# A scan kernel on one core: the Fourier branch's steps at other places of the turn, its loads in one batch a turn

## The chip, the cores and the metric

The kernel runs on one core of a Trainium2 chip. The metric is device time in microseconds (us) of one execution. Five engines work side by side, each through its own list of instructions in a fixed order: TensorE (PE) multiplies matrices, VectorE (DVE) and ScalarE (ACT) do element work, GpSimd (POOL) does element work and issues DMA transfers, SyncE (SP) only issues DMA transfers. An instruction that waits holds up everything behind it on its engine.

## The reference, cut to what matters

One layer of a hybrid backbone over 2048 latent tokens behind a prefix of 256 context tokens. A projection feeds two branches, which are merged by gates, projected and followed by a SwiGLU. The middle of the kernel computes the two branches:

```
S  = S * w_t + (S @ -kk_t) (kk_t * a_t)^T + v_t k_t^T      # branch R: per token, 8 heads of 64,
y  = S @ r_t                                               # forward and backward
f  = real(fftn(u, axes=(row, column, channel)))            # branch F: 32 x 64 grid, 4 groups of 128 channels
m  = sigmoid(gate_f) * (f @ w_up_f) + sigmoid(gate_r) * (rwkv_output(y) @ w_up_r)
```

## The kernel before, in words

The program has four parts: projections (to about 1100 us), the scan (to about 1930 us), the output of the branches, the SwiGLU. The change is in the scan alone.

**The scan.** The tokens are cut into 18 blocks of 128 (2 of context, 16 latent), both directions worked on together. The loop over `s` from -2 to 17 (lines 901 to 958) is a turn. A turn mixes four blocks at different stages: `gram` and `masks` of block `s+2` or `s+3` (PE products `qk`, DVE masks them into QK, POOL stores a part as `ab_dr`), `inv_load` and `invert` (the part comes back as AI; DVE inverts it in 31 small pairs of operations `tm`, `Q`), `inv_store` and `merge_load` (POOL stores `tb_dr<-Q`; SP loads it in another layout as TT and Q2), `merge_a`, `merge_b`, `merge_c` (DVE transposes TT into T; PE `wps`; DVE Wb; PE `t21ps`; ACT writes the result into TT), and a `Chain` for each half block: `x`, `u`, `z`, `state`, `y`, `store`. `state` (DVE, ZC) carries the recurrence from one half to the next. `turn_b` transposes BD on PE into `bt`.

**What sets the order.** All instructions of the scan go through `PE`, `DV`, `AC`, `GP` and `SY`, which keep them in the order in which the code is written (lines 525 to 533). `gn_block` and `gn_open`, which open the part behind the scan in the last turn (lines 904 to 907), are not pinned: a scheduler puts their instructions between.

**The Fourier branch** rides along as a generator, `fourier()`. Each `fill()` of a turn takes one step of it, and there are seven in a turn. First come the steps of 20 units (products `hps`, ACT Dg, products `p12`, ACT q, sums on POOL into fg) and, after each group of five, `halves`: fg is split into a high (`sh`, ACT) and a low half (`sl`, POOL), which SP stores (`fth_dr`, `ftl_dr`, called `ft_dr` in the code). Then come 64 half steps of `pf`: for 4 token blocks `tb` and 8 column blocks `ct`, six products 128x512 each (three for each of two `k`) of a weight tile `wf` (512 KB) with the tiles `fh`, `fl` (256 KB each); after the second half ACT copies pf to `ev`, and SP stores it to `fm_dr`. `defer` puts a store off to a later step, where `flush` issues it. In the code before, each whole `pf` asks for the `wf` three further on, and `ct` 6 and 7 ask for the next `f` tiles, so these loads are spread over the seven places on SP. The numbers in names: `TT8` belongs to block 8, `pf12` to the pair (tb 1, ct 4), `fh2_3` to tb 2 and k 3.

The three places of `fill` behind `merge_a` are lines 950, 955 and 958; the others are 919, 925, 933 and 939. Ahead of each `ch.u()` stands none. Below, "turn 8" is the stretch that begins with the transpose of TT8.

Of the kernel before, what the change touches and what calls it, by code (L numbers as in the profile page):

```python
# [40 lines left out]
def layer_kernel(ctx: ExitStack, tc, I, out_T, dbg=None):  # L41
# [493 lines left out]
    with ExitStack() as st:  # L535
# [237 lines left out]
        def fourier():  # L773
            with tc.tile_pool(name="fd", bufs=1) as fd:
# [8 lines left out]
                def load_x(i):  # L783
                    if i < len(units):
                        g, j0, j1 = units[i]
                        XG[i] = fd.tile([128, 4, 128], F32, tag="xg", name=f"xg{i}", bufs=4)
                        SY.dma_start(XG[i][:, 0:j1 - j0, :], fwv[:, j0:j1, 128 * g:128 * g + 128])
                for i in range(3):
                    load_x(i)

                def adds(fv, q, j0, m):
# [11 lines left out]
                def halves(g, fg, tb):  # L803
                    x = fg.rearrange("p h w -> p (h w)")[:, 512 * tb:512 * tb + 512]
                    hl = [fd.tile([128, 512], F32R, tag=f"s{y}", name=f"s{y}{g}_{tb}", bufs=2) for y in "hl"]
                    AC.activation(out=hl[0], in_=x, func=AF.Copy)
                    GP.tensor_tensor(out=hl[1], in0=x, in1=hl[0].bitcast(F32), op=ALU.subtract)
                    for m in range(2):
                        defer(2, lambda m=m: SY.dma_start(ft_dr[tb][m][:, g, :], hl[m].bitcast(F32)))

                done = None
                for i, (g, j0, j1) in enumerate(units):
                    flush()
                    load_x(i + 3)
                    xg = XG.pop(i)
                    ps = pfl.tile([128, 512], F32, tag="fl", name=f"hps{i}")
                    col = 0
                    for j in range(j0, j1):
                        n = 192 if j == 0 else 128
                        PE.matmul(ps[:, col:col + n], xg[:, j - j0, :], hD0 if j == 0 else hD, start=True, stop=True)  # L820
                        col += n
                    m = col // 64
                    Dg = fd.tile([128, 8, 2, 32], F32, tag="Dg", name=f"Dg{i}")
                    AC.activation(out=Dg.rearrange("p w r h -> p (w r h)")[:, 0:col], in_=ps[:, 0:col], func=AF.Copy)
                    yield
                    if j0 == 0:
                        if done:
                            for tb in range(4):
                                flush()
                                halves(g - 1, done, tb)  # L830
                                yield
                        done = fg = fd.tile([128, 32, 64], F32, tag="fg", name=f"fg{g}")
                    flush()
                    p12 = pfl.tile([128, 2, 256], F32, tag="fl", name=f"p12{i}")
                    for a, w in enumerate((cD, sD)):
                        PE.matmul(p12[:, a, 0:32 * m], w, Dg[:, 0:m, a, :], start=True, stop=True)
                    q = fd.tile([128, 2, 256], F32, tag="q", name=f"q{i}")
                    AC.activation(out=q[:, :, 0:32 * m], in_=p12[:, :, 0:32 * m], func=AF.Copy)
                    defer(1, lambda fg=fg, q=q, j0=j0, m=m: adds(fg.rearrange("p h w -> p w h"), q, j0, m))
                    yield  # L840
                for tb in range(4):
                    flush()
                    if tb == 0:
                        yield
                    halves(3, done, tb)
                    yield
                for _ in range(2):
                    flush()
                    yield
            with tc.tile_pool(name="fx", bufs=1) as fx:  # L850
                FX, WF = {}, {}

                def load_f(tb, k):
                    if tb < 4:
                        FX[tb, k] = [fx.tile([128, 512], F32R, tag=f"f{y}", name=f"f{y}{tb}_{k}", bufs=6) for y in "hl"]
                        for m in range(2):
                            SY.dma_start(FX[tb, k][m].bitcast(F32), ft_dr[TB[tb]][m][:, k, :])

                def load_u(i):
                    if i < 32:  # L860
                        WF[i] = wp.tile([128, KT, 128], F32R, tag="whi" if i % 2 else "wlo", name=f"wf{i}", bufs=2)
                        SY.dma_start(WF[i].bitcast(F32), wf_dr[i % 8])
                for k in range(4):
                    load_f(0, k)
                for i in range(3):
                    load_u(i)
                yield
                for i in range(32):
                    tb, ct = divmod(i, 8)
                    pf = pfl.tile([128, 512], F32, tag="fl", name=f"pf{i}")  # L870
                    for hf in range(2):
                        flush()
                        if hf == 0:
                            load_u(i + 3)
                        if ct == 6 and hf == 0 or ct == 7 and hf:
                            for k in (0, 1) if ct == 6 else (2, 3):
                                load_f(tb + 1, k)
                        w = WF[i]
                        for k in (2 * hf, 2 * hf + 1):
                            xh, xl = FX[tb, k]  # L880
                            for n, (a, x) in enumerate(((k, xh), (k, xl), (4 + k, xh))):
                                PE.matmul(pf, w[:, a, :], x, start=k == 0 and n == 0, stop=k == 3 and n == 2)
                        if hf:
                            ev = fx.tile([128, 512], F32, tag="ev", name=f"ev{i}", bufs=2)
                            AC.activation(out=ev, in_=pf, func=AF.Copy)
                            defer(1, lambda ev=ev, tb=TB[tb], ct=ct: SY.dma_start(fm_dr[ct][:, 512 * tb:512 * tb + 512], ev))
                        yield
                flush()

        fo = fourier()  # L890

# [9 lines left out]
        for s in range(-2, NS):  # L901
# [13 lines left out]
            at(h2, masks, s + 2, 1, 1)  # L915
            at(h2, inv_load, s + 2)
            ch = nxt or Nothing()
            ch.u()
            fill()
            at(h1, invert, s + 1, JA + 3, JA + 10)  # L920
# [39 lines left out]
    pcs.close()  # L960

# [391 lines left out]
```

## Time and profile before

| | us |
|---|---|
| median of 3 runs | 3672.47 (3671.36 to 3676.35) |
| the profiled execution | 3675.67 |
| its span in the trace | 3673.9 |
| transposes of TT0 to TT6 (units of the Fourier branch) | 1169.71 to 1393.44, six turns |
| TT6 to TT7 (the last units, then pf begins) | 1393.44 to 1448.49, one turn |
| TT7 to TT16 (pf) | 1448.49 to 1833.85, nine turns |
| TT16 to TT17 (the last pf, the output part opens) | 1833.85 to 1870.51, one turn |

Over the span PE is busy 91%, DVE 65%, ACT 42%, POOL 19%. The page's mean granted clock of TensorE is 0.933. The program is one long row of turns in its middle, so a transpose of TT ("T") is a good mark: it comes once a turn, on DVE, as soon as TT has come back. A row of a timeline gives in brackets how long the engine had been idle and what released it.

### The profile page before, as it was taken

What the parts mean: (1) busy time and instruction counts of PE and PEld (TensorE: products, weight loads), DVE (VectorE), ACT (ScalarE), POOL (GpSimd) and SP (SyncE); (2) the same over time, 40 slices, a digit from 0 to 9 for tenths busy, and PEclk for the clock granted to TensorE, in tenths of its full rate; (3) what the DMA queues carried; (4) which work ended last, traced back from release to release, by engine and by line L of the source; (5) the groups of instructions that cost most, each with busy time, mean ns of one, the idle gap of its engine ahead of it and who ended that gap; (6) DMA issues with size and microseconds to landing.
All of it is one profiled execution on the core that took longest, in us unless ns stands there. A gap on an engine that the chain in (4) does not pass through costs nothing.

```text
span 3673.9 us, 56433 instructions
## 1 busy us (share of the span) xinstructions
PE 3327.0 (91%) x20612; PEld 2748.4 (75%) x20612; DVE 2398.4 (65%) x4453; ACT 1547.4 (42%) x2896; POOL 688.3 (19%) x1109
## 2 busy tenths in 40 slices
PE   6899799999996887898867998999999899999987
PEld 5777578878885776777756776788878778888876
DVE  5576756655675775566548868877784377777354
ACT  3576555655652443333333325333353233333332
POOL 0133332222232332122115332000020000000000
PEclk9999899999996886889868999999999999999998
DMA  5444645455445656666538765322254532222542
GB/s 184 135 158 139 198 161 181 151 165 176 160 167 161 175 139 175 186 201 211 160 105 315 247 234 175 112 84 81 83 178 137 175 114 81 86 84 74 170 167 100
DMA packets 308373, 568.09 MB, mean 155 GB/s; under 512 B 89696, under 2 KB 100960, under 8 KB 308096
## 3 DMA queue, kind: packets, MB, share of 16 engines
q1 hardware_dynamic: 262000, 418.02, 35.2%
q0 software_dynamic: 46096, 146.47, 12.5%
q8 instruction: 163, 2.67, 0.3%
q14 instruction: 114, 0.93, 0.1%
HBM read 412.68 MB, written 151.67 MB: 154 GB/s over the span
## 4 chain that ended last, share of the span: by engine, by line
PE 63%; issue 14%; DVE 9%; DMA 9%; ACT 3%; POOL 1%; SPq 1%; DVEq 0%; POOLq 0%; ACTq 0%
PE pd L1206 12%; PE fps L161 4%; PE fps L162 4%; PE fps L160 4%; PE pxps L161 3%; PE pxps L162 3%; PE pxps L160 3%; PE pT L160 3%; PE pT L161 2%; PE pT L162 2%; PE qk L531 2%; PE pf L531 2%; DMA TT<-tb_dr 2%; PE pB L160 2%; PE pB L161 2%
## 5 line engine op out<-in xcount | busy, mean ns | idle before, releaser
L154 DVE TENSOR_TENSOR wlo<-wraw,whi 128x512 fp32r<-128x512 f32 x472 | 320.6, 705 | 404.0 <-ACT whi L153 378.5
L153 ACT ACTIVATE whi<-wraw 128x512 fp32r<-128x512 f32 x472 | 282.2, 626 | 477.6 <-PE pd L1206 205.7
L1206 PE MATMUL pd<-uh,whi 128*128 128x512 f32 x704 | 278.3, 396 | 22.6 <-ACT whi L153 21.0
L160 PE MATMUL fps<-hh,whi 128*128 128x512 f32 (+1 forms) x800 | 284.9, 356 | 0.0
L162 PE MATMUL fps<-hh,wlo 128*128 128x512 f32 (+1 forms) x800 | 284.1, 355 | 0.1
L161 PE MATMUL fps<-hl,whi 128*128 128x512 f32 (+1 forms) x800 | 281.5, 352 | 0.0
L1206 PE MATMUL pd<-ul,whi 128*128 128x512 f32 x704 | 277.0, 393 | 0.0
L160 PE MATMUL pxps<-hh,whi 128*128 128x512 f32 (+2 forms) x720 | 250.1, 348 | 19.8 <-ACT hh L232 9.4
L1206 PE MATMUL pd<-uh,wlo 128*128 128x512 f32 x704 | 254.9, 392 | 0.4 <-DVE wlo L154 0.3
L161 PE MATMUL pxps<-hl,whi 128*128 128x512 f32 (+2 forms) x720 | 246.5, 343 | 6.0 <-DVE hl L233 5.8
L162 PE MATMUL pxps<-hh,wlo 128*128 128x512 f32 (+2 forms) x720 | 245.4, 344 | 2.0 <-DVE wlo L154 1.9
L1144 DVE TENSOR_TENSOR u<-u,pT 128x512 f32<-128x512 f32 x176 | 120.9, 687 | 143.5 <-PE pT L162 141.7
L1154 POOL DMA_DIRECT2D u_dr<-u x44 | 23.9, 544 | 842.5 <-DVE u L1153 794.2
L1206 PEld LDWEIGHTS pd<-uh,whi 128*128 128x128 f32 x704 | 134.1, 191 | 55.7 <-ACT whi L153 24.7
L531 DVE TENSOR_TENSOR tm<-Q,AI 128x126 f32<-128x126 f32 (+22 forms) x558 | 150.5, 270 | 33.2 <-DMA AI<-ab_dr 16.0
L161 PEld LDWEIGHTS fps<-hl,whi 128*128 128x128 f32 x800 | 151.7, 190 | 25.0 <-issue 5.8
L162 PEld LDWEIGHTS fps<-hh,wlo 128*128 128x128 f32 x800 | 151.6, 190 | 24.6 <-issue 3.9
L160 PEld LDWEIGHTS fps<-hh,whi 128*128 128x128 f32 x800 | 152.1, 190 | 23.8 <-issue 4.3
L160 PEld LDWEIGHTS pxps<-hh,whi 128*128 128x128 f32 x720 | 137.6, 191 | 41.2 <-ACT hh L232 11.3
L531 DVE TENSOR_TENSOR Q<-Q,tm 128x126 f32<-128x126 f32 (+22 forms) x558 | 147.2, 264 | 20.1
L161 PEld LDWEIGHTS pxps<-hl,whi 128*128 128x128 f32 x720 | 137.5, 191 | 27.0 <-DVE hl L233 8.6
L1206 PEld LDWEIGHTS pd<-uh,wlo 128*128 128x128 f32 x704 | 133.1, 189 | 29.2 <-DVE wlo L154 1.3
(703 smaller groups left out, 8628.7 us busy)
## 6 DMA issues: line engine op xcount, KB each, us to landing
wraw<-w_in SPq DMA_DIRECT2D x210, 256.0 KB, 3.3
wraw<-w_down SPq DMA_DIRECT2D x176, 256.0 KB, 2.9
wA<-w_gu SPq DMA_DIRECT2D x176, 256.0 KB, 2.7
BD<-bd_dr SPq DMA_DIRECT2D x36, 512.0 KB, 6.7
KR<-kr_dr SPq DMA_DIRECT2D x36, 512.0 KB, 7.4
wada<-w_ada SPq DMA_DIRECT2D x32, 512.0 KB, 4.2
wraw<-w_out SPq DMA_DIRECT2D x64, 256.0 KB, 3.0
wf<-wf_dr SPq DMA_DIRECT2D x32, 512.0 KB, 5.7
```

Source lines behind the costliest of these rows:

```text
L153: nc.scalar.activation(out=hi[:, k0:k1, :], in_=raw, func=AF.Copy)
L154: nc.vector.tensor_tensor(out=lo[:, k0:k1, :], in0=raw, in1=hi[:, k0:k1, :].bitcast(F32), op=ALU.subtract)
L160: nc.tensor.matmul(ps, wh[:, k, :], xh(k), start=start and k == 0, stop=False)
L161: nc.tensor.matmul(ps, wh[:, k, :], xl(k), start=False, stop=False)
L162: nc.tensor.matmul(ps, wl[:, k, :], xh(k), start=False, stop=stop and k == K - 1)
L531: return lambda *a, **k: tc.keep_in_program_order(f(*a, **k))
L1144: nc.vector.tensor_tensor(out=o, in0=x, in1=y, op=ALU.add)
L1154: nc.gpsimd.dma_start(u_dr[f][:, TT[hf]:TT[hf] + 512], c)
L1206: nc.tensor.matmul(PD[ct], x[:, ct, :], y, start=f == 0 and i == 0, stop=f == FT - 1 and i == 2)
```

## The change

It does six things. (1) The seven `fill` places move: one ahead of the first `ch.u`, one behind each `ch.u`, one behind the first `ch.store`, one behind `merge_load` and `load_v`, one between `invert(10, 12)` and `merge_a`, and one (instead of three) behind `merge_a`. (2) The loads of `wf` and `f` are no longer asked for by each step but once a turn, right behind `merge_a` in the code, by `ahead[0]`; a step asks itself only for what is still missing. (3) The `xg` tiles have 3 buffers instead of 4 and are loaded 2 units ahead instead of 3. (4) Dg and q have two buffers. (5) `halves` go two to a step, with more empty steps around them. (6) The `f` tiles have 7 buffers instead of 6.

```diff
-                for i in range(3):
+                for i in range(2):
                     load_x(i)
@@ fourier(), the units
-                    Dg = fd.tile([128, 8, 2, 32], F32, tag="Dg", name=f"Dg{i}")
+                    Dg = fd.tile([128, 8, 2, 32], F32, tag="Dg", name=f"Dg{i}", bufs=2)
...
                             for tb in range(4):
                                 flush()
                                 halves(g - 1, done, tb)
-                                yield
+                                if tb % 2:
+                                    yield
@@ fourier(), pf
+                def loads(i):
+                    for j in range(i, i + 4):
+                        load_u(j)
+                    load_f(i // 8, 4)
+                    load_f(i // 8 + 1, 3)
+                load_f(0, 4)
+                loads(0)
...
-                        if hf == 0:
-                            load_u(i + 3)
-                        if ct == 6 and hf == 0 or ct == 7 and hf:
-                            for k in (0, 1) if ct == 6 else (2, 3):
-                                load_f(tb + 1, k)
...
+                        ahead[0] = lambda j=i + hf: loads(j)
                         yield
@@ the turn
             ch = nxt or Nothing()
+            fill()
             ch.u()
             fill()
...
             ch.store()
-            fill()
             at(h1, merge_load, s + 1)
             at(h1, load_v, s + 1, 1)
+            fill()
...
             at(h2, invert, s + 2, 10, 12)
+            fill()
             at(h1, merge_a, s + 1)
+            at(ahead[0], lambda: ahead[0]())
             at(h2, turn_b, s + 2, 0, 1)
             fill()
             at(h3, gram, s + 3, 0, 0)
             at(h2, invert, s + 2, 12, JA)
             at(h1, merge_b, s + 1)
             at(h2, turn_b, s + 2, 1, 0)
-            fill()
             at(h3, gram, s + 3, 0, 1)
             at(h2, turn_b, s + 2, 1, 1)
-            fill()
```

On PE, between the transposes `bt12_1_0` behind merge_a of block 11 and the products `qk13_0_1`, before:

```order
L531 MATMUL bt12_1_0_15918<-cn_132,BD12_1_15167 128x128 x4
L531 MATMUL pf14_15873<-fh1_2_14894,wf14_15410 128x512
L531 MATMUL pf14_15873<-fl1_2_14895,wf14_15410 128x512
L531 MATMUL pf14_15873<-fh1_2_14894,wf14_15410 128x512
L531 MATMUL pf14_15873<-fh1_3_14898,wf14_15410 128x512
L531 MATMUL pf14_15873<-fl1_3_14899,wf14_15410 128x512
L531 MATMUL pf14_15873<-fh1_3_14898,wf14_15410 128x512
L531 MATMUL qk13_0_1_0_15932<-KR13_0_15671,BD13_0_15669 128x128
L531 MATMUL qk13_0_1_1_15933<-KR13_0_15671,BD13_0_15669 128x128
```

and in the changed kernel:

```order
L531 MATMUL bt12_1_0_15948<-cn_132,BD12_1_15193 128x128 x4
L531 MATMUL qk13_0_1_0_15954<-KR13_0_15699,BD13_0_15697 128x128
L531 MATMUL qk13_0_1_1_15955<-KR13_0_15699,BD13_0_15697 128x128
L531 MATMUL qk13_0_1_0_15954<-KR13_0_15699,BD13_0_15697 128x128
L531 MATMUL qk13_0_1_1_15955<-KR13_0_15699,BD13_0_15697 128x128
L531 MATMUL qk13_0_1_0_15954<-KR13_0_15699,BD13_0_15697 128x128
```

The six products of one fill no longer stand there; the same holds behind `bt12_1_1`.

On SP, from the load of TT10 on to the load of AI12 and what follows, before:

```order
L531 DMA TT10_15280<-tb_dr0_92 32x16x32 x4
L531 DMA Q210_15282<-tb_dr0_92 128x8x32
L531 DMA UV10_1_0_15292<-v_dr_72 64x512
L531 DMA UV10_1_1_15294<-v_dr_72 64x512
L531 DMA fm_dr2_100<-ev10_15373 128x512
L531 DMA wf14_15410<-wf_dr6_120 128x1024
L531 DMA AI12_15502<-ab_dr0_90 64x1024 x2
L531 DMA fm_dr3_101<-ev11_15440 128x512
L531 DMA wf15_15530<-wf_dr7_121 128x1024
```

and in the changed kernel:

```order
L531 DMA TT10_15296<-tb_dr0_92 32x16x32 x4
L531 DMA Q210_15298<-tb_dr0_92 128x8x32
L531 DMA UV10_1_0_15308<-v_dr_72 64x512
L531 DMA UV10_1_1_15310<-v_dr_72 64x512
L531 DMA fm_dr2_100<-ev10_15222 128x512
L531 DMA wf12_15393<-wf_dr4_118 128x1024
L531 DMA wf13_15395<-wf_dr5_119 128x1024
L531 DMA wf14_15397<-wf_dr6_120 128x1024
L531 DMA wf15_15399<-wf_dr7_121 128x1024
L531 DMA fm_dr3_101<-ev11_15378 128x512
L531 DMA AI12_15524<-ab_dr0_90 64x1024 x2
```

Four `wf` go out together behind TT10, and `wf12`, which the first step behind merge_a reads, is among them; before, `wf14` and `wf15` were asked for here.

On DVE, in turn 16 (the operations `tm17` and `Q17` invert block 17, `gny` and `s8` are of `gn_block`), before:

```order
L531 TENSOR_TENSOR Q17_18069<-Q17_18069,tm17_14_18441 128x8x17
L531 TENSOR_TENSOR tm17_15_18444<-Q17_18069,AI17_18068 128x8x16
L531 TENSOR_TENSOR Q17_18069<-Q17_18069,tm17_15_18444 128x8x16
L531 TENSOR_TENSOR Wb16_0_18447<-wps16_0_18411,cn_132 128x512
L531 TENSOR_TENSOR Wb16_1_18449<-wps16_1_18412,cn_132 128x512
L531 TENSOR_TENSOR tm17_16_18483<-Q17_18069,AI17_18068 128x9x15
```

and in the changed kernel, where thirteen rows of `gn_block` stand ahead of Wb16_0 (the last of them here):

```order
L496 TENSOR_TENSOR gny_18807<-gny_18807,s8_18815 128x512
L501 RECIPROCAL s8_18780<-s8_18780 128x8
L502 TENSOR_TENSOR gny_18772<-gny_18772,s8_18780 128x512
L498 TENSOR_REDUCE s8_18815<-gnb_18808 128x8
L531 TENSOR_TENSOR Wb16_0_18449<-wps16_0_18421,cn_132 128x512
L499 TENSOR_SCALAR s8_18815<-s8_18815 128x8
L531 TENSOR_TENSOR Wb16_1_18451<-wps16_1_18422,cn_132 128x512
```

Wb16_0, which followed the inversion directly, now stands behind work on tiles that `gn_block` loads.

## Rows read from the trace of the kernel before

**Rows 1.** Busy time by stretch: us, PE, PEld, DVE, ACT, POOL, PEclk, DMA share, GB/s.

```profile
1393.00:1448.00 55.00, 37.11 (x454) 33.09 (x452) 26.89 (x78) 18.07 (x43) 13.30 (x19) 0.62 0.67 192
1621.00:1665.00 44.00, 37.94 (x474) 31.25 (x474) 26.14 (x79) 16.37 (x39) 8.26 (x15) 0.88 0.76 228
```

**Rows 2.** Timeline of DVE: start us, us, engine, instruction, [idle before <- what released it].

```profile
1169.71 1.43 DVE L531 STREAM_TRANSPOSE T<-TT 32x512 f32<-32x512 f32 x2 [3.95 <-DMA TT<-tb_dr]
...
1393.44 0.70 DVE L531 STREAM_TRANSPOSE T<-TT 32x512 f32<-32x512 f32 x1 [3.58 <-DMA TT<-tb_dr]
...
1448.49 1.43 DVE L531 STREAM_TRANSPOSE T<-TT 32x512 f32<-32x512 f32 x2 [14.45 <-DMA TT<-tb_dr]
...
1620.95 1.50 DVE L531 STREAM_TRANSPOSE T<-TT 32x512 f32<-32x512 f32 x2 [3.85 <-DMA TT<-tb_dr]
...
1645.42 0.69 DVE L531 TENSOR_TENSOR ZC<-pz,ZC 128x512 f32<-128x512 f32 x1 [2.44 <-PE pz L531]
...
1664.72 1.51 DVE L531 STREAM_TRANSPOSE T<-TT 32x512 f32<-32x512 f32 x2 [6.56 <-DMA TT<-tb_dr]
...
1833.85 1.43 DVE L531 STREAM_TRANSPOSE T<-TT 32x512 f32<-32x512 f32 x2 [1.72 <-DMA TT<-tb_dr]
1837.84 1.28 DVE L531 TENSOR_TENSOR Wb<-wps,cn 128x512 f32<-128x512 f32 x2
1849.01 0.69 DVE L493 TENSOR_TENSOR gny<-gny,gnb 128x512 f32<-128x512 f32 x1 [3.83 <-DMA gnv<-bv_dr]
...
1870.51 1.43 DVE L531 STREAM_TRANSPOSE T<-TT 32x512 f32<-32x512 f32 x2
```

**Rows 3.** Timeline of PE in turn 11, from T at 1620.95.

```profile
1622.60 1.12 PE L531 MATMUL wps<-T,LT 32*128 32x128 f32 x14 [0.35 <-DVE T L531]
...
1631.74 0.47 PE L531 MATMUL pf<-fh,wf 128*128 128x512 f32 x1
...
1633.31 1.16 PE L531 MATMUL qk<-KR,BD 64*128 64x128 f32 x16
...
1638.78 2.06 PE L531 MATMUL pu<-X,TT 64*64 64x64 f32 x32 [1.32 <-issue]
1640.78 0.79 PE L531 MATMUL pf<-fh,wf 128*128 128x512 f32 x1
...
1643.64 1.73 PE L531 MATMUL pz<-UV,BT 128*64 128x64 f32 x32
...
1654.38 1.15 PE L531 MATMUL pz<-UV,BT 128*64 128x64 f32 x32
```

**Rows 4.** Timeline of POOL in turns 10 and 11.

```profile
1609.22 1.62 POOL L531 DMA_DIRECT2D tb_dr<-Q  x2 [1.78 <-DVE Q L531]
...
1649.41 1.62 POOL L531 DMA_DIRECT2D tb_dr<-Q  x2 [1.02 <-DVE tm L531]
```

**Rows 5.** Timeline of SP in turns 6, 11 and 16.

```profile
1433.30 0.32 SPq L531 DMA_DIRECT2D fh<-fth_dr  x1
...
1440.38 3.81 SPq L531 DMA_DIRECT2D TT<-tb_dr  x4
...
1449.08 0.58 SPq L531 DMA_DIRECT2D wf<-wf_dr  x1
...
1642.21 1.09 SPq L531 DMA_DIRECT2D AI<-ab_dr  x2
...
1655.57 0.59 SPq L531 DMA_DIRECT2D wf<-wf_dr  x1
...
1839.61 0.33 SPq L531 DMA_DIRECT2D fm_dr<-ev  x1
1843.74 0.33 SPq L518 DMA_DIRECT2D g<-g  x1
```

**Rows 6.** Tiles wf: from issue to landing.

```profile
DMA to landing us min/median/max: 3.7/5.7/10.4
```

**Rows 7.** Tiles fth_dr, stores of sh and loads of fh: from issue to landing.

```profile
DMA to landing us min/median/max: 2.0/5.4/10.6
```

More of the change, by code (lines that the diff above doesn't have):

```diff
@@ L785, in load_x @@
                         g, j0, j1 = units[i]
-                        XG[i] = fd.tile([128, 4, 128], F32, tag="xg", name=f"xg{i}", bufs=4)
+                        XG[i] = fd.tile([128, 4, 128], F32, tag="xg", name=f"xg{i}", bufs=3)
                         SY.dma_start(XG[i][:, 0:j1 - j0, :], fwv[:, j0:j1, 128 * g:128 * g + 128])
-                for i in range(3):
+                for i in range(2):
                     load_x(i)
@@ L813, in fourier @@
                     flush()
-                    load_x(i + 3)
+                    load_x(i + 2)
                     xg = XG.pop(i)
@@ L827, in fourier @@
                         if done:
+                            flush()
+                            yield
                             for tb in range(4):
@@ L830, in fourier @@
                                 halves(g - 1, done, tb)
-                                yield
+                                if tb % 2:
+                                    yield
                         done = fg = fd.tile([128, 32, 64], F32, tag="fg", name=f"fg{g}")
@@ L836, in fourier @@
                         PE.matmul(p12[:, a, 0:32 * m], w, Dg[:, 0:m, a, :], start=True, stop=True)
-                    q = fd.tile([128, 2, 256], F32, tag="q", name=f"q{i}")
+                    q = fd.tile([128, 2, 256], F32, tag="q", name=f"q{i}", bufs=2)
                     AC.activation(out=q[:, :, 0:32 * m], in_=p12[:, :, 0:32 * m], func=AF.Copy)
                     defer(1, lambda fg=fg, q=q, j0=j0, m=m: adds(fg.rearrange("p h w -> p w h"), q, j0, m))
[L840 to L845, printed above, removed]
                     yield
@@ L849, in fourier, with load_f @@
                     yield
+                for tb in range(4):
+                    flush()
+                    halves(3, done, tb)
+                    if tb % 2:
+                        yield
+                for _ in range(4):
+                    flush()
+                    yield
             with tc.tile_pool(name="fx", bufs=1) as fx:
                 FX, WF = {}, {}
[L853 to L857, printed above, removed]
+                def load_f(tb, n):
+                    for k in range(n):
+                        if tb < 4 and (tb, k) not in FX:
+                            FX[tb, k] = [fx.tile([128, 512], F32R, tag=f"f{y}", name=f"f{y}{tb}_{k}", bufs=7) for y in "hl"]
+                            for m in range(2):
+                                SY.dma_start(FX[tb, k][m].bitcast(F32), ft_dr[TB[tb]][m][:, k, :])
                 def load_u(i):
-                    if i < 32:
+                    if i < 32 and i not in WF:
                         WF[i] = wp.tile([128, KT, 128], F32R, tag="whi" if i % 2 else "wlo", name=f"wf{i}", bufs=2)
                         SY.dma_start(WF[i].bitcast(F32), wf_dr[i % 8])
[L863 to L866, printed above, removed]
+                def loads(i):
[5 more added lines that the diff above has]
+                loads(0)
+                yield
                 yield
@@ L869, in fourier @@
                     tb, ct = divmod(i, 8)
+                    load_u(i)
+                    load_f(tb, 4)
                     pf = pfl.tile([128, 512], F32, tag="fl", name=f"pf{i}")
@@ L886, in fourier @@
                             defer(1, lambda ev=ev, tb=TB[tb], ct=ct: SY.dma_start(fm_dr[ct][:, 512 * tb:512 * tb + 512], ev))
+                        ahead[0] = lambda j=i + hf: loads(j)
                         yield
+                ahead[0] = None
                 flush()
+        ahead = [None]
         fo = fourier()
```

## The prediction, made before the changed kernel ran

> **What bounds the kernel now.** I first read where the changed code runs. Everything ahead of the first turn and behind the last keeps its order, so only the stretch from 1169.71 to T17 at 1870.51 and the work just behind it can move. I cut it at the transposes of TT on DVE [rows 2]: 223.7 us for the six turns with units (37.3 each), 55.1 for turn 6, 385.4 for the nine pf turns 7 to 15 (1448.49 to 1833.85, 42.8 each), 36.7 for turn 16.
>
> Next, one pf turn in time: turn 11, 43.8 us from T at 1620.95 to T at 1664.72 [rows 2]. The cycle that closes it: T, wps on PE 1.65 later, then PE without a gap through bt, qk and three fills to t21ps; ACT writes TT, for which PE stops 1.32; pu, a fill, pz [rows 3]; ZC on DVE at 1645.42, T+24.5; inverse operations until POOL stores tb_dr at 1649.41 [rows 4], 4.0 behind ZC; the trip through memory and back into TT, 15.3, and the next T. Two things bound the turn: this cycle, and PE's own work, which is not far below: 37.9 busy of the 44 in the window [rows 1]. DVE has 26.1, ACT 16.4, POOL 8.3 there and bound nothing.
>
> The trip is not constant. For TT11 it was 11.7 (1609.22 to 1620.95), for TT12 15.3 [rows 2, 4]; ahead of TT12, SP issued a wf of 512 KB at 1655.57 [rows 5]. The mean turn, 42.8 less 24.5 less 4.0, gives a mean trip of 14.3.
>
> In turn 6 the chain has another limit: T7 waited 14.45 on its load [rows 2]. SP had stood until 1433.30, for the last store of ft, and then issued eight f and three wf before TT at 1440.38 [rows 5], which landed at T7 only: 3.6 MB in 15.2 us, about 240 GB/s.
>
> **The pf turn without a late load.** One fill of PE at full clock is 1.57 (1631.74 to 1633.31), one at low clock 2.86 (1640.78 to 1643.64) [rows 3]. Two fills between T and t21ps go: -3.1. The new fill ahead of `ch.u` falls into PE's wait of 1.32 for TT and costs about 0.2. It also keeps PE running there. The fill between pu and pz should then take about 1.5 instead of 2.86, and pz 1.15 as at 1654.38, not 1.73: -1.4 and -0.6. So ZC stands at T+19.4 (24.5 less 5.1). With 4.0 to the store and a trip of 12 (nearer to 11.7 since no wf is issued just ahead of TT any more) the cycle would close at 35.4. PE's floor is a little higher: 37.94 [rows 1], less 1.3 and 0.6 of low clock, plus 0.35 of the wait in front of wps [rows 3], is 36.4. A turn that waits for no load is 36.4, against 42.8.
>
> **The late loads.** The batch goes out behind TT, Q2 and UV; the first wf behind UV in turn 7 went out at 1449.08 [rows 5], T+0.6, and with fm ahead I take T+1. A wf lands 5.7 later (median; 3.7 to 10.4) [rows 6], so at T+6.7. In most turns the step behind merge_a reads a wf of the batch before. Counting seven steps a turn against two steps a wf, this fails in turns 8, 10, 12 and 14: there wf5, wf12, wf19 and wf26 are first asked for in the batch behind TT and read by the one fill behind merge_a, at T+3.1 (wps starts at T+1.65, [rows 3]). PE then stops 3.6, and behind it qk, masks and t21ps; with a little more low clock I take 3.8, ends 1.6 (lands in 3.7) and 8.3 (10.4). Such a turn is 40.2. Two smaller cases: in turn 9 fh1_3 goes out in the batch for a step soon after, +1. In turn 11 fh2_3, asked for by the first step of the next turn's set, stands behind AI13 on SP. AI is issued when the second masks are stored, T+21.3 before (1642.21, [rows 5]), so T+18.2 with two fills less, and fh2_3 behind it at T+19.3; it lands at T+24.7 by the median of 5.4 [rows 7]. The fill behind `ch.u` reads it at T+17.5: +7 (ends 4 and 12).
>
> Nine turns: four of 40.2, turn 9 at 37.4, turn 11 at 43.4, three of 36.4, together 350.8. Against 385.4: **-34.6**.
>
> **Turn 6.** The stores of the last halves begin earlier, and the eight f, four wf and six f of the next block go out behind TT6, not ahead of TT7. That is 5.8 MB, and the BD and KR of the turn (2.1 MB) stand behind it, then TT7. At the stretch's 192 GB/s [rows 1] 7.9 MB take 41 us from T+2: T7 at T+43 in place of 55.1, **-12**. At 240 GB/s it would be 35 and PE's floor of 36.4 decides (-19); if the stores still hold SP up it stays 55 (0). Here the Trainium skill speaks against a batch: "DMA: Bandwidth & Descriptors", Queues, rings and completion order, gives every queue one ring on each DMA engine, which is drained packet by packet, so AI8, BD9, KR9 and TT7, which SP issues on the same queue behind the batch, would wait for its bytes. The trace agrees where TT, issued at 1440.38 behind eleven loads, was only there at 1448.49. By that rule the 43 holds, and without it the turn would be 36.4; the sum above rests on the rows alone.
>
> **The turns with units.** Fewer steps stand between T and t21ps there too, but each unit's step is short, and the turns are at 37.3, 0.9 above a pf turn's floor: 5 us at most to gain in six turns, 8 with the low clock. Against it: sh has two buffers, so the third half (now in the step right behind the first two) waits on ACT for a store that lands 5.4 later [rows 7], with X and BT behind it, and POOL's sl with tb_dr behind it. Twice 5.4 or 10.6, where T waited 3.95 and 3.58 for TT [rows 2], so some 4 of slack each: +3 to +12. I take 0, ends -8 and +12. The buffers of xg, Dg and q I cost at nothing: a unit's loads are asked for a step later but the unit's products lie beside DVE's inverse; if that cover were gone, one load of about 5 at the start.
>
> **Turn 16.** Before, Wb16 stands at T+4.0 (1837.84), and the first gny at T+15.2, waiting for gnv [rows 2]. These loads go out behind the last fm store at 1839.61 and g2 at 1843.74 [rows 5]. Now thirteen rows of gn_block stand ahead of Wb16_0. Even with the last pf done two fills earlier, g2 leaves at about T+6.5, its loads land by T+11 and the thirteen rows take some 6: Wb16 at T+18, 14 later than before. DVE's inverse and PE's work fill some of it: T17 at T+46 instead of 36.7. Behind T17 the same gn work is then done, which gives about 5 back: **+5**, ends 0 and 12.
>
> Sum: -34.6 -12 +0 +5 = -42. From the profiled execution's 3675.7 it is 3634, and from the median of 3672.5, 3.2 below it, **3631**.
>
> **Rivals.**
> 1. *Late loads at their worst.* Four wf at once on the queues land as the slowest did, 10.4, not 5.7: 4.7 more in turns 8, 9, 10, 12 and 14, and 5.2 in turn 11, +29, so 3660. For it: the batch is four times what went out together; DMA already has a share of 0.76 in a pf turn [rows 1]. Against it: at T+1 the batch has little beside it.
> 2. *Loads land early.* The spread load's 5.7 includes BD, KR and f beside it; alone behind TT it lands in 3.7. Then four stalls shrink by 2.0, turn 9's goes, turn 11's shrinks by 3.4: -12, 3619. The Trainium skill, "DMA: Bandwidth & Descriptors", Anatomy of one DMA, fits 2.0 us plus bytes / 436e3, by which 512 KB would take an estimated 3.2; it is written for GpSimd's path, and the median here, 5.7, does not agree.
> 3. *The steps were not on the path.* PE's floor, not the cycle, makes the turn: the seven fills only stand elsewhere, the pf turns stay at 42.8, turn 6 gives 12, the turns with units 3, turn 16 takes 5: -10, 3662. For it: PE is busy 37.9 of 44. Against it: PE stopped 1.32 for TT [rows 3], and DVE stood 3.85 and 6.56 before T [rows 2].
> 4. *Slower: the stretch from T to ZC falls to low clock.* With two fills less behind merge_a PE waits for wf and then for TT, and its granted clock, 0.62 in turn 6 where PE waits [rows 1], comes down for the whole stretch. Its work there is some 17 us (ZC at T+19.4 less the waits), at low clock about 1.7 times as long (2.86 to 1.57, 1.73 to 1.15 [rows 3]): +12, of which 3 are paid already, so 9 above the forecast's turn. Six turns so would be +54: 3685. From five turns on, the gain of 42 is gone. For it: four turns have the late wf. Against it: the stops are about as long as the waits of before; after T's of 3.85 [rows 2] the fill at 1631.74 ran at full clock again [rows 3].
>
> **How the numbers follow.** The forecast has 0.55, with its own range of 3612 to 3650 (ends of the stalls and of turns 6 and 16). Late loads 0.15, early loads 0.08, not on the path 0.10, low clock 0.12. 0.2% is 7.3 us, about what can be told from no change, so "faster" lies below 3665. Faster: 0.55, 0.08, 0.13 of the late loads, 0.06 of rival 3: 0.82. The same: 0.02, 0.04 and 0.02 of rival 4, 0.08. Slower: 0.10 of rival 4. The range for 8 in 10 reaches from 3605 (early loads with turn 6 at its floor) to 3664 (rivals 1 and 3).
>
> **What would show it.** T to T of 36 to 37 in turns 7, 13 and 15 and about 40 in 8, 10, 12 and 14, with PE's wait for wf in front of the first pf behind wps; ZC at T+19 to 20; pz at 1.15 and no low clock at pu; turn 11 with a wait for fh or fl behind pu; T7 at 43 behind T6; Wb16 behind the gn rows. The prediction is wrong if pf turns without a late load stay above 40, if T to ZC runs at low clock, or if turn 6 is no shorter.

## The result, and the profile after

The changed kernel takes 3630.8 us (median of four runs, 3628.84 to 3634.34) against 3671.9 for the kernel before (3663.07 to 3676.35). The ratio is 0.9892 with a 95% interval of 0.9872 to 0.9912: about 1.1%, or 41 us, less. The forecast was 3631, the range 3605 to 3664.

The time was right to 1 us, and that is luck: several of its terms were off, and their errors cancel. The scan cut at the transposes of TT, and behind it up to the first product `pr` of the output part (first row at 1924.41 before, 1881.57 after):

| stretch | before | forecast | after |
|---|---|---|---|
| turns 0 to 5 (units) | 223.7 | 223.7 | 219.7 |
| turn 6 | 55.1 | 43 | 42.4 |
| turns 7 to 15 (pf) | 385.4 | 350.8 | 341.3 |
| T16 to the first pr | 90.6 | 95.6 | 107.7 |

T0 came 0.8 later, and what is behind pr was 2.1 shorter; the six differences (+0.8, -4.0, -12.6, -44.0, +17.1, -2.1) make up, to rounding, the 44.9 between the two spans, 3673.9 and 3629.0.

**The pf turns.** First the windows: us, busy PE, PEld, DVE, ACT, POOL, the granted clock of TensorE, the share and rate of DMA. The nine pf turns before:

```profile
1448.49:1833.85 385.36, 341.99 (x4230) 282.48 (x4230) 232.82 (x702) 140.51 (x332) 74.36 (x135) 0.86 0.62 184
```

The nine after, then turn 13, turn 15 and turn 11 alone:

```profile
1432.59:1773.91 341.32, 311.10 (x4243) 255.31 (x4239) 232.20 (x702) 142.55 (x337) 73.64 (x134) 0.95 0.69 201
...
1667.23:1701.79 34.56, 33.99 (x476) 28.11 (x475) 25.84 (x79) 15.76 (x39) 8.25 (x15) 1.00 0.76 218
1742.69:1773.91 31.22, 29.21 (x417) 24.18 (x415) 25.65 (x78) 14.47 (x35) 7.72 (x14) 1.00 0.65 182
1583.01:1624.99 41.98, 34.22 (x432) 27.73 (x430) 25.91 (x78) 14.56 (x35) 7.94 (x15) 0.88 0.62 178
```

The same matmuls, 0.3% apart in their number, took 342.0 us before and 311.1 after. Of the 44.0 that the nine turns lost, 30.9 is PE taking less time for them (granted clock 0.86, then 0.95) and 13.2 is PE standing less. In turn 13 the clock is at full speed throughout, and PE works 34.0 of 34.6 us.

What PE waited for is the other half of the reading. Waits of PE in the nine turns before (what waits, for what: us in total, times, longest):

```profile
PE wps L531 <- DVE T L531: 38.9, 12, 10.3
PE pu L531 <- issue: 11.8, 9, 1.3
```

and after:

```profile
PE pf L531 <- DMA wf<-wf_dr: 15.4, 4, 4.6
PE pf L531 <- DMA fh<-fth_dr: 8.8, 2, 7.5
PE xr L531 <- DVE ZC L531: 1.8, 1, 1.8
PE wps L531 <- DVE T L531: 1.1, 4, 0.3
```

The waits for T and those in front of pu are gone. What is left are the late loads that the prediction named. They stand in turns 8, 10 and 11 as follows (timeline of PE after, in the columns of [rows 3]); turns 12 and 14 have the same row with 3.10 and 4.59:

```profile
1475.76 0.77 PE L531 MATMUL pf<-fh,wf 128*128 128x512 f32 x1 [3.60 <-DMA wf<-wf_dr]
...
1550.91 0.77 PE L531 MATMUL pf<-fh,wf 128*128 128x512 f32 x1 [4.09 <-DMA wf<-wf_dr]
...
1606.19 0.79 PE L531 MATMUL pf<-fh,wf 128*128 128x512 f32 x1 [7.53 <-DMA fh<-fth_dr]
```

Turn 13, which waits for no load, on DVE, and at pz on PE:

```profile
1667.23 0.70 DVE L531 STREAM_TRANSPOSE T<-TT 32x512 f32<-32x512 f32 x1 [4.01 <-DMA TT<-tb_dr]
...
1684.87 0.69 DVE L531 TENSOR_TENSOR ZC<-pz,ZC 128x512 f32<-128x512 f32 x1
...
1701.79 1.47 DVE L531 STREAM_TRANSPOSE T<-TT 32x512 f32<-32x512 f32 x2 [4.22 <-DMA TT<-tb_dr]
```

```profile
1680.96 1.15 PE L531 MATMUL pu<-X,TT 64*64 64x64 f32 x32
...
1683.64 1.15 PE L531 MATMUL pz<-UV,BT 128*64 128x64 f32 x32
```

ZC stands at T+17.6, where turn 11 before had T+24.5 [rows 2]; pu takes 1.15 instead of 2.06 and has no wait, pz 1.15 instead of 1.73 [rows 3]. DVE waits 4 us for T, and PE does not notice: its steps of pf stand there now.

**Turn 6.** T7 waited 14.45 before [rows 2]. After, the timelines of DVE, of ACT, of PE, of SP and of POOL:

```profile
1390.19 0.70 DVE L531 STREAM_TRANSPOSE T<-TT 32x512 f32<-32x512 f32 x1 [2.89 <-DMA TT<-tb_dr]
...
1423.34 0.19 DVE L531 TENSOR_TENSOR tm<-Q,AI 128x31 f32<-128x31 f32 x1 [3.38 <-DMA AI<-ab_dr]
...
1432.59 1.43 DVE L531 STREAM_TRANSPOSE T<-TT 32x512 f32<-32x512 f32 x2 [1.29 <-DMA TT<-tb_dr]
```

```profile
1387.38 0.63 ACT L531 ACTIVATE sh<-fg 128x512 fp32r<-128x512 f32 x1 [4.72 <-DMA fth_dr<-sh]
1389.04 0.63 ACT L531 ACTIVATE sh<-fg 128x512 fp32r<-128x512 f32 x1 [1.03 <-DMA fth_dr<-sh]
1389.69 1.32 ACT L531 ACTIVATE Y<-xr 64x256 f32<-64x256 f32 x4
```

```profile
1390.80 3.94 PE L531 MATMUL xr<-ZC,KR 64*128 64x64 f32 x32 [4.41 <-ACT Y L531]
```

```profile
1378.43 0.45 SPq L531 DMA_DIRECT2D fth_dr<-sh  x1
...
1409.99 0.32 SPq L531 DMA_DIRECT2D fl<-ftl_dr  x1
1417.90 1.24 SPq L531 DMA_DIRECT2D AI<-ab_dr  x2
```

```profile
1411.34 1.29 POOL L531 DMA_DIRECT2D ab_dr<-QK  x2 [3.44 <-DVE tm L531]
```

TT7 is hardly waited for. But ACT stands for a store of `sh` issued at 1378.43, until 1387.38, and then for the next one; Y comes late, PE starts the turn 4.4 late and at low clock (3.94 for the 32 products of xr, 2.00 in turn 11 before; the granted clock of the first 21.8 us of the turn is 0.66). Later DVE stands for AI8. SP issued it 6.6 behind POOL's last two stores of ab_dr, with the batch on the queues; in turn 13 it was 3.0 (1681.15 to 1684.18). The experiments take these apart.

**Turn 16.** DVE and PE, to be read against 1837.84 and 1849.01 of [rows 2]:

```profile
1786.35 0.69 DVE L493 TENSOR_TENSOR gny<-gny,gnb 128x512 f32<-128x512 f32 x1 [8.03 <-DMA sg<-sg_dr]
```

```profile
1776.67 1.16 PE L531 MATMUL wps<-T,LT 32*128 32x128 f32 x16
1790.88 1.12 PE L531 MATMUL bt<-cn,BD 128*128 128x128 f32 x4 [13.05 <-ACT BT L531]
1795.36 1.11 PE L531 MATMUL bt<-cn,BD 128*128 128x128 f32 x4 [3.37 <-ACT BT L531]
```

DVE reaches gny at T16+4.4 and stands 8.0 for its loads with Wb16 behind it. On ACT a square of gn_block stands ahead of BT17, so PE stands 13.0 as well (timeline of ACT):

```profile
1788.78 0.63 ACT L497 ACTIVATE gnb<-gny 128x512 f32<-128x512 f32 x1 [12.22 <-DVE gny L496]
1789.43 0.77 ACT L531 ACTIVATE X<-xr 64x256 f32<-64x256 f32 x2
1790.22 0.60 ACT L531 ACTIVATE BT<-bt 128x512 f32<-128x512 f32 x1
```

T17 comes 50.6 behind T16, not 46. Branch F has no step left here: its last product pf is 5.1 ahead of T16, where before it was 4.7 behind.

### The profile page after: what moved, and what is told of

It is laid out like the page before. It is cut to its first block, busy times and chain, and to the rows that moved or that the text cites. A ratio compares the mean times of both kernels' runs of the same rounds, so it can differ in the third digit from the quotient of the medians.

```text
span 3629.0 us, 56399 instructions
## 1 busy us (share of the span) xinstructions
PE 3295.6 (91%) x20612; PEld 2720.0 (75%) x20612; DVE 2405.6 (66%) x4453; ACT 1546.9 (43%) x2896; POOL 692.0 (19%) x1109
## 4 chain that ended last, share of the span: by engine, by line
PE 39%; DVE 4%; issue 3%; DMA 3%; ACT 1%; POOL 0%; SPq 0%; DVEq 0%; ACTq 0%; POOLq 0%
PE pd L1219 12%; PE pT L160 4%; PE pT L161 4%; PE pT L162 4%; PE pB L160 3%; PE pB L161 3%; PE pB L162 3%; PE po L162 1%; PE po L161 1%; PE po L160 1%; DVE wlo L154 1%; DMA wraw<-w_down 1%; DMA wr<-wr_dr 1%; DMA gny<-y_dr 0%; DMA gf<-g_dr 0%
## 5 line engine op out<-in xcount | busy, mean ns | idle before, releaser
L531 DVE TENSOR_TENSOR tm<-Q,AI 128x126 f32<-128x126 f32 (+22 forms) x558 | 150.5, 270 | 40.4 <-DMA AI<-ab_dr 23.7
L160 PEld LDWEIGHTS pxps<-hh,whi 128*128 128x128 f32 x720 | 138.5, 193 | 40.6 <-ACT hh L232 11.3
```

The costliest lines, as they stand in the source:

```text
L160: nc.tensor.matmul(ps, wh[:, k, :], xh(k), start=start and k == 0, stop=False)
L531: return lambda *a, **k: tc.keep_in_program_order(f(*a, **k))
```

## The experiments

Each run was timed beside the kernel before on the same chip; the ratio to it has its 95% interval in brackets. The stretches come from one profile of each run. The kernel before had medians from 3671.9 to 3677.1 beside these runs, so the ratios, and not the medians, are what compares runs that are close.

| kernel | median us, ratio | turns 0-5 | turn 6 | turns 7-15 | T16 to pr |
|---|---|---|---|---|---|
| before | 3671.9 | 223.7 | 55.1 | 385.4 | 90.6 |
| changed | 3630.8, 0.9892 (0.9872-0.9912) | 219.7 | 42.4 | 341.3 | 107.7 |
| places alone | 3662.0, 0.9970 (0.9955-0.9986) | 237.0 | 53.5 | 363.8 | 97.3 |
| batch alone | 3657.4, 0.9954 (0.9940-0.9968) | 230.4 | 57.3 | 371.7 | 92.4 |
| places and batch, old units | 3661.7, 0.9967 (0.9953-0.9981) | 237.8 | 57.7 | 349.0 | 97.5 |
| batch behind the fill | 3597.0, 0.9790 (0.9771-0.9809) | 223.3 | 40.6 | 314.8 | 99.9 |
| gn's first add in order | 3623.4, 0.9856 (0.9840-0.9872) | 218.2 | 41.2 | 348.4 | 107.0 |
| halves a step apart | 3634.6, 0.9885 (0.9866-0.9904) | 215.7 | 42.5 | 345.7 | 105.1 |
| these three | 3604.8, 0.9808 (0.9785-0.9831) | 220.5 | 42.1 | 314.2 | 105.1 |
| batch ahead of TT | 3661.6, 0.9974 (0.9957-0.9992) | 223.5 | 39.4 | 379.3 | 107.5 |
| last halves in free buffers | 3639.9, 0.9906 (0.9884-0.9929) | 220.1 | 40.9 | 350.6 | 106.9 |
| and six f later | 3630.1, 0.9874 (0.9850-0.9897) | 223.9 | 37.2 | 347.3 | 107.3 |
| and the batch behind the fill | 3593.5, 0.9777 (0.9751-0.9803) | 223.7 | 36.5 | 314.5 | 101.0 |
| and gn later | 3587.3, 0.9765 (0.9743-0.9787) | 217.1 | 36.6 | 318.2 | 106.2 |

The five kernels that have the changed kernel's pf turns unaltered (changed, gn's add, halves apart, free buffers, six f later) show 341.3 to 350.6 for turns 7 to 15. So 9 us there is what one profile differs from another, and the changed kernel's 341.3 is the lowest of them.

**The places alone**, in the kernel before:

```diff
+            fill()
             ch.u()
...
-            fill()
             at(h1, merge_load, s + 1)
             at(h1, load_v, s + 1, 1)
+            fill()
...
             at(h2, invert, s + 2, 10, 12)
+            fill()
...
-            fill()
...
-            fill()
```

The last two lines that go are the second and third place behind `merge_a`.

> The kernel before with only the seven places moved; its loads and units are the old ones. Theory A (the places shorten the way from T to ZC, the batch of loads only pays in turn 6): pf turns of 36 to 38, ZC at T+18 to 20 and no wait for wf behind merge_a, nine turns of about 335 against 385; turn 6 still near 55, since SP still stands for the last store of ft; the time about 3672 - 45 = 3627. Rival B (the gain is the trip that loses the wf ahead of TT; the places are neutral): pf turns stay at 41 to 43 and the time at 3660 to 3675.

Theory A was right on ZC (T+19.8 in the mean of the nine turns, T+24.5 before), on the missing wait for wf and on turn 6, and wrong on the sum: 40.4 a turn, not 36 to 38. The time, 3662.0, lies in rival B's range, but B's reason is refuted by ZC. What ZC gains, the trip takes back in part: a turn less ZC less 4.0 is 16.6 here, 14.3 before. And the units lost 13. Before, ACT reached the third half of turn 0 when the chain's UV was done (timeline of ACT before):

```profile
1186.66 1.21 ACT L531 ACTIVATE UV<-pu 64x512 f32<-64x512 f32 x2 [2.29 <-PE pu L531]
1193.13 0.63 ACT L531 ACTIVATE sh<-fg 128x512 fp32r<-128x512 f32 x1 [5.26 <-DMA fth_dr<-sh]
```

Now it stands ahead of UV (timelines of ACT and of PE in this run):

```profile
1195.20 0.63 ACT L531 ACTIVATE sh<-fg 128x512 fp32r<-128x512 f32 x1 [9.10 <-DMA fth_dr<-sh]
1195.85 1.21 ACT L531 ACTIVATE UV<-pu 64x512 f32<-64x512 f32 x2
```

```profile
1197.11 1.97 PE L531 MATMUL pz<-UV,BT 128*64 128x64 f32 x32 [7.25 <-ACT UV L531]
```

ACT waits 9.1 for the store that frees the buffer, PE's pz 7.2 for ACT, and ZC is at T+27.8. The store took only 4.4 of it: SP issued it at 1190.82, behind AI, which it could issue at 1189.64 (timeline of SP):

```profile
1189.64 1.09 SPq L531 DMA_DIRECT2D AI<-ab_dr  x2
1190.82 0.54 SPq L531 DMA_DIRECT2D fth_dr<-sh  x1
```

Turns 0, 2 and 4 wait in the same way (9.0 to 9.3, where before it was 5.3 to 6.3) and are 43.0, 45.3 and 43.1, against 36.1, 40.1 and 38.0.

**The batch alone**, in the kernel before: the new `loads`, called behind merge_a.

> The kernel before with only the loads in one batch behind merge_a (and 7 buffers of f); its places and units are the old ones. Theory A: ZC stays at T+24, the trip falls to about 12, so turns that wait for no wf are 40 to 41, but four wait some 4 us for one; turn 6 stays at 50 to 60, as the old units store ft late; the time 3665 to 3685. Rival B: pf turns of 36 to 38 without the new places, the time about 3635 to 3645.

In the pf turns A held on ZC (T+25.3) and on the trip (12.0), at 41.3 a turn; of the four late wf there is one (2.2), but two waits for fh (8.1). The time, 3657, lies below A's 3665 and far above B's. The profiles of this run and of the places alone, at 3667.7 and 3669.8, are each the slowest of ten times, so the 15 us that this run's median gained cannot be placed in a stretch. Within what one profile differs from another, the pf turns add up: -21.6 for the places, -13.7 for the batch, and -36.4 with both and the old units. PE's busy time in them, 342.0 before, is 326.4, 338.0 and 315.1 in these three runs, at a granted clock of 0.91, 0.87 and 0.93: the faster products come mainly with the places.

**Both, with the units of before:**

```diff
-                        XG[i] = fd.tile(..., bufs=3)
+                        XG[i] = fd.tile(..., bufs=4)
...
                                 halves(g - 1, done, tb)
-                                if tb % 2:
-                                    yield
+                                yield
```

Not shown: Dg and q go back to one buffer, the loads of `xg` to 3 units ahead, and the empty steps around the halves to those of before.

> The changed kernel with the units of before (xg 4 buffers, Dg and q one, halves one at a time, no extra steps). Theory A (the earlier stores of the last halves make turn 6): turn 6 back to 50 to 55 from 42.4, the pf turns at the changed kernel's mean of 38, so the time about 3640 to 3645. Rival C (the batch behind TT6 makes turn 6, whatever the units do): turn 6 at 42, the time at 3631.

Rival C is out. Turn 6 is at 57.7, and the units are at 237.8 as with the places alone, so A's price was too low. The new units, which the prediction priced at nothing in turns 0 to 5, are worth some 18 us there and 15 in turn 6: with the new places and the batch but the old units only 11 us of the 41 are left. That the halves two at a time do it, and not the buffers or the empty steps that changed with them, is likely but not shown: ACT's waits for a store of sh in turns 0 to 5 are 27.9 here and 13.0 in the changed kernel.

**The batch one place later:**

```diff
-            at(ahead[0], lambda: ahead[0]())
             at(h2, turn_b, s + 2, 0, 1)
             fill()
+            at(ahead[0], lambda: ahead[0]())
```

> The changed kernel with the batch of loads one place later, behind the fill that follows merge_a, so that a wf whose buffer that fill frees can go along. Theory A (late loads are what the pf turns still lose): no wait for wf in turns 8, 10, 12, 14 (15.4 us in the changed kernel's trace), none for fh in turns 9 and 11 (1.3 and 7.5), turns at 34 to 36.4, the time 3631 - 24 to 3631 - 30, so 3601 to 3607. Rival D (PE's own work is the floor at 36.4 and fills the gap): under 10 gained, 3621 to 3631.

A held, and a little more than it asked for: 3597. The fill behind merge_a ends the use of one wf, so the batch behind it can carry one more, which the next fill behind merge_a finds there; the last f goes along too. The waits of PE for wf are gone and those for fh and fl down to 1.7; the turns fall to a mean of 35.0. The window of the nine turns:

```profile
1431.68:1746.49 314.81, 305.42 (x4249) 252.35 (x4249) 231.82 (x703) 141.88 (x336) 72.97 (x133) 0.98 0.73 218
```

PE is now busy 97% at a clock of 0.98: it bounds these turns. Of the 34 us between the two medians, 26.5 lie in them by the two profiles; 7.8 lie between T16 and pr, and why is not shown.

**gn's first add kept in the written order**, behind Wb17:

```diff
-        nc.vector.tensor_tensor(out=y, in0=y, in1=yb, op=ALU.add)
+        first = nc.vector.tensor_tensor(out=y, in0=y, in1=yb, op=ALU.add)
+        if i // 4 == TB[0]:
+            tc.keep_in_program_order(first)
```

> The changed kernel with the first add of gn_block kept in the written order on DVE, so that its rows stand behind Wb17 and no longer ahead of Wb16. Theory A (turn 16 is long because Wb16 and BT17 stand behind gn work that waits for its loads): turn 16 from 50.6 to 33 to 37, Wb16 at T+4, and of this 0 to 4 lost behind T17, where all of the gn work is then done; the time 3631 - 10 to 3631 - 17, so 3614 to 3621. Rival E (the gn work is the limit wherever it stands): what turn 16 gives comes back behind T17, the time 3626 to 3636.

Wb16 is at T+4.0, turn 16 falls to 33.1, and T17 to pr rises from 57.0 to 73.9 (timeline of DVE):

```profile
1774.48 1.43 DVE L533 STREAM_TRANSPOSE T<-TT 32x512 f32<-32x512 f32 x2
1778.46 1.28 DVE L533 TENSOR_TENSOR Wb<-wps,cn 128x512 f32<-128x512 f32 x2
...
1807.59 1.43 DVE L533 STREAM_TRANSPOSE T<-TT 32x512 f32<-32x512 f32 x2
...
1861.40 0.69 DVE L533 TENSOR_TENSOR ZC<-pz,ZC 128x512 f32<-128x512 f32 x1 [8.09 <-PE pz L533]
```

ZC17 is 53.8 behind T17 (38.7 after the change). T16 to pr is 107.0 and 107.7, the same, as rival E had it. The time, 3623.4, lies between the ranges of A and E; the 7 us by which the median is lower are not in that stretch.

**The last halves a step apart:** `if tb == 1: flush(); yield` between the pairs, one empty step less behind them.

> The changed kernel with one empty step between the two pairs of the last halves (and one less behind them). Theory F (turn 6 is still at 42.4 because ACT's sh waits 4.7 and 1.0 for stores, Y and PE's xr stand behind it, and wps begins 6 late at low clock): no such wait, turn 6 at 36 to 38, the time 3631 - 4 to 3631 - 6. The prediction's own reason (7.9 MB ahead of TT7 at 192 GB/s): turn 6 stays at 41 to 43, the time at 3631.

Turn 6 stays at 42.5. It does not refute F: the wait only moved. The last sh waits 5.84 for its store one place later, with X and BT behind it, and DVE then stands 6.47 for AI8. The time, 3634.6, is above F's range and is the changed kernel's within the intervals.

**All three at once.**

> The changed kernel with the batch behind the fill, the first add of gn_block in the written order and the last pairs of halves a step apart, all three. If the three gains add up: pf turns 315 as with the late batch alone, turn 16 at 33 to 37, turn 6 at 35 to 38, the time 3597 - 12 to 3597 - 20, so 3577 to 3585. If turn 16 and turn 6 are limited elsewhere: 3590 to 3600.

The gains of the pf turns are there (314.2), the other two are not, as in the single runs. The time, 3604.8, is above both ranges and not below that of the batch behind the fill alone (3597.0; the intervals overlap).

**The batch ahead of TT:**

```diff
+            at(ahead[0], lambda: ahead[0]())
             at(h1, merge_load, s + 1)
...
-            at(ahead[0], lambda: ahead[0]())
```

> The changed kernel with the batch on SP ahead of TT instead of behind it. Theory A (what stands ahead of TT on SP lengthens the trip; a load needed right behind merge_a comes late only because it is asked for behind TT): no wait for wf, but TT lands 4 to 9 later in every pf turn, turns of 40 to 44, the time 3640 to 3665. Rival G (the bytes pass beside each other, only the asking was too late): turns of 34 to 36.4 as with the batch behind the fill, the time about 3600.

The time is in A's range and G is out, but A was wrong that no wf is waited for. PE waits 25.0 for wf, seven times, most of it in the fill that now follows load_v. TT pays too: T10 stood 7.6 behind the issue of its TT at 1589.47 (1597.03), T14 of the changed kernel 4.3 (1697.52 to 1701.79); in the mean of the nine turns it is 7.8 here and 3.8 there. Of the 7.2 a turn by which this run is above the batch behind the fill, 5.6 are the way from POOL's store of tb_dr to the next T (17.3 against 11.6) and 1.5 the way from T to ZC (20.6 against 19.1).

**Turn 6 taken apart.** First the last two halves in the buffers of Dg and q, which are free by then:

```diff
-  hl = [fd.tile([128, 512], F32R, tag=f"s{y}", ...) for y in "hl"]
+  free = g == 3 and tb >= 2
+  hl = [fd.tile([128, 512], F32R, tag={"h": "Dg", "l": "q"}[y] if free else f"s{y}", ...) for y in "hl"]
```

> The changed kernel with the last two halves of the last group written into the buffers of Dg and q, which are free by then, so that neither sh nor sl waits for a store of ft. Theory F (the waits of sh on ACT are what keeps turn 6 at 42.4): no wait of ACT for a store around T6, turn 6 at 36 to 38, the time 3631 - 4 to 3631 - 6. Theory H (what bounds turn 6 is the batch: AI8 is issued behind its last f and DVE stands for it ahead of ZC): turn 6 at 40 to 43, DVE waits 4 or more for AI8, the time 3628 to 3634.

ACT waits for no store there, ZC is at T+20.2 instead of T+26.1, and still turn 6 is 40.9: DVE stands for AI8 instead. SP issues it at 1412.92, 7.9 behind POOL's last two stores of ab_dr at 1405.07, and it is there 9.9 later. The time, 3639.9, is above both ranges; the ratio is that of the changed kernel within the intervals.

```profile
1422.78 0.19 DVE L531 TENSOR_TENSOR tm<-Q,AI 128x31 f32<-128x31 f32 x1 [9.09 <-DMA AI<-ab_dr]
```

Then also the six f of the next block out of the first batch (`if i: load_f(i // 8 + 1, 3)`):

> The same, and the six f of the next block left out of the first batch (they go with the next one), 1.6 MB less between TT6 and AI8. Theory H: AI8 is issued at T+19 to 21 instead of T+27 and turn 6 is 36 to 38, turn 7 no longer than 38; the time 5 below that of the run with the halves in free buffers. Theory F: no difference between the two.

Turn 6 is 37.2, and DVE's wait for AI8 shorter (the last two stores at 1406.84, issue 6.7 later at 1413.56, there 7.5 later):

```profile
1421.04 0.19 DVE L531 TENSOR_TENSOR tm<-Q,AI 128x31 f32<-128x31 f32 x1 [5.57 <-DMA AI<-ab_dr]
```

So both theories were half of it: the wait of sh and that for AI8 lay one behind the other. AI8's place on SP was the smaller part of theory H (it went out at T+21.5 here, at T+23.2 with the six f): the store that it waits for and its own load are both slow while the batch is on the queues. POOL's four stores of ab_dr in turn 6 took 2.3 to 2.4 to land before, and 5.3 to 6.6 in the changed kernel and in these two runs, with the lighter batch as well. The two parts of the load took 8.3 and 8.5 with the six f ahead of them, 6.3 and 6.9 without (3.7 and 4.5 in the changed kernel, where they went out 7.9 behind the last f, not 2.8). The Trainium skill's rule on rings ("DMA: Bandwidth & Descriptors", Queues, rings and completion order), cited in the prediction, bears on this load, which SP issues behind the batch, and the trace agrees in that it was shorter by 2 behind the lighter batch. It does not bear on the store, which goes out from POOL. Turn 7 at 39.0 was 1 above what was expected.

**The best two.** With the batch behind the fill as well:

> That, and the batch behind the fill. If the gains add up: pf turns at 315 as with the late batch alone, turn 6 at 36 to 38, the time 3597 - 4 to 3597 - 8, so 3589 to 3593.

The time, 3593.5, is as expected to 0.5, but its interval and that of the batch behind the fill alone overlap. Then gn_block's first two blocks written behind `u` of block 16 (and `gn_open`, with the end of branch F, ahead of them), the other two behind `state` of block 17, and their first adds kept in that order:

> That, and gn_block's first two blocks written behind u of block 16, the other two behind the state of block 17, with their first adds kept in that order on DVE. Theory E (the four blocks of gn are 17 us dearer than before because their work no longer lies beside pf and waits in front of the chain): T16 to the first pr 88 to 95 instead of 100 with the late batch, the time 3580 to 3588. If the work is the limit wherever it stands: 98 to 107, the time as without it or up to 8 above.

The time is in theory E's range, but not for its reason: turn 16 and the way to pr did not get shorter (106.2). The median, 3587.3, is the lowest of all, at a ratio of 0.9765 to the kernel before, and beats the changed kernel; against the version before it the intervals overlap, and the 6 us would lie behind the first pr.

## Why the prediction was right, and where its steps were not

On the total it was right by luck. By the two profiles the pf turns came 9.5 lower than forecast, the units 4.0 and turn 6 0.6, and the way from T16 to pr 12.1 higher. What was right for its reason are the late loads, the two parts of the cycle and the earlier stores in turn 6.

**The late loads: right in place and size.** The forecast named turns 8, 10, 12 and 14 with 3.8 and turn 11 with 7; PE waited 3.60, 4.09, 3.10, 4.59 and 7.53; in turn 9, forecast with 1, it was 1.28. The four turns are 38.5 to 42.2, forecast 40.2. Neither rival 1 nor rival 2 came. The tiles wf after, to be read against [rows 6], land 1.4 later in the median, but none in 10.4 and none in 3.7; the estimate of 3.2 from the Trainium skill ("DMA: Bandwidth & Descriptors", Anatomy of one DMA) is met by none:

```profile
DMA to landing us min/median/max: 5.0/7.1/8.8
```

**ZC and the trip: right.** ZC at T+17.5 to 18.8 in turns 7, 13 and 15 (forecast 19.4). The trip of 12 is borne out by the batch alone, 12.0 with the old places, and by the batch behind the fill, 11.9 with hardly a late load (1.7). The places alone shorten the way to ZC, the batch alone the trip.

**PE's floor: wrong.** 36.4 was called the least a turn can take. Turn 13 took 34.6, the mean with the batch behind the fill is 35.0. The step that failed took low clock off the 37.94 of [rows 1] at two places only, the fill and pz behind pu; in the window the clock was 0.88 and other instructions ran low too, the first fill behind wps (2.50 from 1624.07 to 1626.57) and pu (2.06) among them. With the granted clock at 1.00, turn 13 after, a turn is 34.0 of work. Taken nine times, the 1.9 that the prediction took off are 17; PE's busy time fell by 30.9. Turn 15, at 31.2, holds a step or so of pf less, since the branch ends in it. Turn 15 alone is 5.2 of the 9.5 by which the nine turns came lower than forecast, and that in the lowest of five profiles.

**Turn 6: the right number from half the reason.** That the stores of the last halves begin earlier was right, as turn 6 is back at 57.7 with the old units. Bytes ahead of TT7 at 192 GB/s were then to make it 43. But TT7 was hardly waited for (1.29), and the queues moved 280 GB/s there. The batch slowed AI8 and the store ahead of it, and the wait of sh for its store, priced under the units, lay in front of that.

**The units: near the right number from two wrong ones.** Called 0, measured -4. The wait of sh on ACT was named as a risk of the changed halves. It was there before (17.5 in turns 0 to 5), but behind UV; the new places put it ahead of UV and made it 27.5, and with the old units turns 0 to 5 were 13 longer. The new units took that away again (-18).

**Turn 16: the term that was mis-sized.** +5 was forecast with an end of 12, and it was +17 up to pr. Wb16 came at T+20, as rows of gn_block that wait for loads stand ahead of it. The 5 said to be given back behind T17 were not: T17 to pr is 57.0 against 53.9. Two of the four blocks of gn start behind T17 and ahead of ZC17 in both kernels, so there was nothing to give back. Why 90.6 is not reached again is open: moving gn by one add (107.0) or to two other places (106.2) did not do it. One rival was not tested, that branch F ends too early: in the three kernels with pf left in turn 16 (before, batch alone, old units) Wb16 stands at T+4.0 to 5.3 and T16 to pr is 90.6 to 97.5; in those with none it is 97.3 to 107.7.

**The other rivals.** "Not on the path" is refuted by the places alone in the pf turns, -21.6. "Low clock" came out the other way round over the nine turns: the granted clock rose, and PE's busy time fell by 31 of the 44 us. In small it is there: from T to ZC the granted clock is 0.85 to 0.93 in the four turns with a late wf and 1.00 in turn 13, and for about as many products (201 and 203 against 203) turns 8 and 14 have 0.9 and 2.2 us more of busy PE, where the rival asked for 9.

**The prediction's sums** hold to rounding but for two. ZC at T+19.4 leaves out the 0.2 of the new fill, and early loads with turn 6 at its floor are 3619 less 7, 3612, not 3605.

## What to carry to other kernels

Put the filler work of an engine where it would stand for something else, and price it at the clock: here the same products took 31 us less when PE's stops in front of T (38.9 us) and of pu (11.8) were gone. Loads that go out in one batch belonged here behind the small load that the chain waits for, and behind the last use that frees one more buffer: ahead of TT the batch took away most of the gain (3662), and one place further back was worth 34 us (3631 to 3597). Where a store must free a buffer, the engine that fills it next waits: look at what stands behind it on that engine before the work is moved.

## What the runs showed of the hardware that had not been expected

- A store of 256 KB that goes out right behind BD and KR (2.1 MB) held its buffer for 9.0 us (1378.43 to 1387.38 in turn 5 after), where the stores of sh and loads of fh together have a median of 4.4 in that run.
- A transfer beside a batch slows as well: the two parts of AI8 (64x1024 elements each) took 8.3 and 8.5 from issue to landing with the last halves in free buffers, and 6.3 and 6.9 without the six f; the median of all AI is 4.1 and 4.2 in these runs. The stores of ab_dr ahead of it, issued by POOL, took 5.5 to 6.6 and 5.3 to 6.6, against 2.3 to 2.4 in turn 6 before.
- Two waits in a row do not add: in turn 6 the one taken away alone gave 1.5 us (42.4 to 40.9, no more than profiles of the unaltered turn differ, 41.2 with gn's first add in order), and with the lighter batch it was 5.2 (37.2).
- With nothing to wait for, the granted clock stayed at 1.00 over whole turns of 34.6 and 31.2 us, with PE busy 98% and 94%; over the nine turns it was 0.98 with the batch behind the fill, 0.95 in the changed kernel and 0.86 before.
